# A hybrid decoder layer on one NeuronCore: products with the values in groups of four query blocks

## The chip, the core and the metric

The kernel runs on one core of one Trainium2 chip. The metric is device time in microseconds (us). TensorE multiplies matrices and transposes; the profile shows its matmuls as PE and its weight loads as PEld. VectorE (DVE), ScalarE (ACT) and GpSimd (POOL) work on what it leaves in its banks (PSUM) and on tiles in the core's memory (SBUF). SyncE (SP) and POOL issue DMAs. Each engine works through its own instructions in program order.

## What is computed

One layer on a sequence of 1024 rows of width 1024, all in fp32: a norm, one wide projection, two kinds of attention side by side, an output projection, a norm and the residual. The change touches the first kind, differential attention, with 8 heads:

```python
def diff_attention(q, k, v, lam):
    # q, k: per head two maps of 64 columns; v: per head 128 columns
    ...
        s = jnp.einsum('bqhmd,bkhmd->bhmqk', qb, k).astype(jnp.float32)
        ...
        p = jax.nn.softmax(jnp.where(mask, s, -jnp.inf), axis=-1)
        w = p[:, :, 0] - lam * p[:, :, 1]
        return jnp.einsum('bhqk,bkhv->bqhv', w.astype(v.dtype), v)
...
    oa = rms_norm(oa, subln_g) * (1.0 - lam_init)
    oa = oa.reshape(B, S, DA_WIDTH) * jax.nn.silu(ga)
```

The mask is causal: query row i sees keys 0 to i. So of the 8 x 8 squares of 128 queries by 128 keys that a head has, the 36 on and under the diagonal are computed.

## The kernel before

**Precision.** TensorE is fed with a split of each fp32 factor into a high part (`hi`, rounded to the matmul's type) and the rest (`lo`). A product is three matmuls: hi x hi, lo x hi, hi x lo. ACT makes the high part (a cast), DVE the rest (a subtraction).

**Stages.** Up to about 617 us of the profile the projections run, and the second attention (gated linear attention) beside them. Then comes the stage that the change touches, up to about 933 us, and then the end, which completes the output projection and the last norm.

**The stage.** Three streams share TensorE there, each a Python generator that issues instructions and yields what they cost:

- `all_scores` goes through the heads and, in a head, through the query blocks `qb` from 7 down to 0. `scores(h, qb)` makes the scores of 128 queries against (qb + 1) x 128 keys for both maps (matmuls `sc`), DVE finds each row's extreme while it copies the scores out (a custom instruction, L1167, and a read of its accumulator), ACT takes the exponential with the row sum (L1177), and `scale_scores` joins the maps: DVE a reciprocal (L1202), POOL one product (L1203), DVE the other and the difference (L1207). The result stays in `p0`, one buffer per `qb`; `w[h, qb]` names it.
- `all_values` takes `w` to the products with the values. `values(h, j, ...)` handles the pair of query blocks 2j and 2j + 1. In `turn(g)` TensorE transposes up to four squares of 128 x 128 (two key blocks by two query blocks) into one bank (`wtr`, L114, two banks in rotation, `TR`), ACT casts it to `wt_hi` (L1244) and DVE subtracts to `wt_lo` (L1245). `times(g, ...)` multiplies the two key blocks of v with them: six matmuls into the bank `po`, of 256 columns each, or 128 for the key block that only one of the two query blocks sees. Each turn is issued ahead of the products of the turn before it (`ready`). ACT then copies `po` to half of `o` (L1272). `attn_norm` normalizes `o`, 512 queries at a time: a square and a cast on ACT, a subtraction on DVE (`sq_hl`, L1285), a sum over partitions by two matmuls with ones (`ms`, in the next `TR` bank), a logarithm and an exponential on ACT, products on DVE and POOL, and a store to `mixd`.
- `out_early` multiplies parts of the output projection whose inputs are ready (`ypart`, three matmuls of 512 columns for each step). It waits for nothing of the other two for most of the stage.

**What sets the order.** `merge` holds a clock for each stream and always advances the one that is furthest behind; a stream runs from its begin to its end time (the first two numbers of its list), and each yielded cost moves its clock by that share. A yielded function is a condition that holds a stream back until it is true. So `LAG` sets how far the values follow the scores: 21 of the clock's units, where a head takes 36. `used` tells the scores that a pair's buffers have been read, so that the next head may write them. TensorE's instructions are kept in the order in which they are issued (`mm`, `tr`). The order on ACT, DVE and POOL is settled when the program is built.

Of the kernel before, what the change touches and what calls it, by code (L numbers as in the profile page):

```python
# [14 lines left out]
P = 128  # L15
# [5 lines left out]
DA_HEADS = 8  # L21
# [10 lines left out]
def hymba_kernel(  # L32
# [65 lines left out]
    def bank(i, shape, name):  # L98
        return psum.tile(shape, F32, tag=f"b{i}", name=name)
# [1037 lines left out]
    w, used, scored, opened = {}, set(), [], {}  # L1137

# [73 lines left out]
    def all_scores():  # L1212
        for h in range(DA_HEADS):
            for qb in range(NT - 1, -1, -1):
                if qb % 2 and h:
                    yield lambda h=h, qb=qb: (h - 1, qb // 2) in used
                yield from scores(h, qb)
                if qb == NT - 1 and h + 1 < DA_HEADS:
                    for n, half in (("q", 1), ("k", 0), ("k", 1), ("qs", 1)):
                        load_qk(h + 1, n, half)  # L1220
            if h + 1 < DA_HEADS:
                for n in ("q", "qs"):
                    load_qk(h + 1, n, 0)
        for _ in range(3):
            scale_scores(None)
        scored.append(True)
        opened.update(dict.fromkeys(SC))

    def values(h, j, v, o):

        yield lambda: (h, 2 * j) in w
        po = bank(PO, [P, 256], "po")

        def turn(g):

            n = 512 if g < j else 384
            pt = tr_bank("wtr", [P, 512])
            for c in range(0, n, P):
                t, i = (c // 256, c % 256 // P) if c < 256 or g < j else (1, 1)
                kt = 2 * g + t  # L1240
                tr(pt[:, c : c + P], w[h, 2 * j + i][:, kt * P : (kt + 1) * P])
            hi = smp.tile([P, 512], F32R, tag="wt_hi", name="wt_hi", bufs=3)
            lo = smp.tile([P, 512], F32R, tag="wt_lo", name="wt_lo", bufs=3)
            act.copy(hi[:, :n], pt[:, :n])  # L1244
            dve.tensor_tensor(lo[:, :n], pt[:, :n], fp(hi[:, :n]), ALU.subtract)  # L1245
            return hi, lo

        def times(g, wt):
            hi, lo = wt
            for i, t in ((0, 0), (1, 0), (0, 1), (1, 1), (2, 0), (2, 1)):  # L1250
                a, b = ((v[0], hi), (v[1], hi), (v[0], lo))[i]
                kt = 2 * g + t
                ns = 256 if kt <= 2 * j else P
                mm(
                    po[:, 256 - ns :], a[:, kt, :], b[:, 256 * t : 256 * t + ns],
                    start=(kt == 0 and i == 0), stop=(kt >= 2 * j and i == 2),
                    skip_group_check=True,
                )

        ready = []  # L1260
        for g in range(j + 1):
            ready.append((g, turn(g)))
            if g == j:
                used.add((h, j))
            yield 0.5
            if len(ready) > 1:
                times(*ready.pop(0))
                yield 0.5
        if j == 0:
            yield 0.5  # L1270
        times(*ready.pop(0))
        act.copy(o[:, j % 2 * 256 : j % 2 * 256 + 256], po)  # L1272
        yield 0.5
# [45 lines left out]
    def all_values():  # L1319
        carry = iter(())  # L1320
        nxt = v_first
        for h in range(DA_HEADS):
            v = nxt
            o = [smp.tile([P, 512], F32, tag="o", name="o", bufs=3) for _ in range(2)]
            yield from mingle(values(h, 3, v, o[1]), carry)
            if h + 1 < DA_HEADS:
                nxt = load_v(h + 1)
            yield from values(h, 2, v, o[1])
            yield from mingle(
                chain(values(h, 1, v, o[0]), values(h, 0, v, o[0])), attn_norm(h, 1, o[1])  # L1330
# [170 lines left out]
    def last_times(st, dh, part, e):  # L1501
# [9 lines left out]
    LAG = 21.0  # L1511
# [6 lines left out]
        [LAG, T + LAG, DA_HEADS * 10.5, all_values()],  # L1518
# [128 lines left out]
```

## Time and profile before

| | |
|---|---|
| median of 3 runs | 976.23 us (976.2 to 981.91) |
| the profiled execution's own time | 977.73 us |
| its span, first to last instruction | 976.0 us |
| TensorE clock granted | 0.998 of full speed |
| PE busy | 956.0 us, 98% of the span, 4866 matmuls |
| PEld busy | 806.1 us, 83% |
| DVE busy | 738.7 us, 76% |
| ACT busy | 590.9 us, 61% |
| POOL busy | 211.5 us, 22% |

A matmul's busy time contains its passage through the array, which overlaps with the next one's. What a matmul costs the stream is the time from its start to the start of the next, and that is read from the timeline. A wait of TensorE shows as a wait of PE, or of PEld where the weight load had to wait.

### The profile page before, as it was taken

The numbers are of one execution on the slowest core, as the hardware profiler recorded it, in microseconds if no ns is written. First come the engines' busy times: TensorE is split into PE (matmuls) and PEld (weight loads), VectorE is DVE, ScalarE is ACT, GpSimd is POOL, SyncE is SP. The second block draws the span as 40 slices with busy tenths as digits, with TensorE's granted clock in tenths as the row PEclk, the third lists the DMA queues.
The fourth block names the chain that finished last, engine by engine and source line by source line (L and its number), as shares of the span: only waits on it lengthen the run. The fifth ranks groups of instructions, "written<-read, shape, count | busy, mean of one in ns | idle before, by whom it ended". The sixth has DMA issues, their size and how long they took to land.

```text
span 976.0 us, 14803 instructions
## 1 busy us (share of the span) xinstructions
PE 956.0 (98%) x4866; PEld 806.1 (83%) x4866; DVE 738.7 (76%) x1450; ACT 590.9 (61%) x1152; POOL 211.5 (22%) x289
## 2 busy tenths in 40 slices
PE   6999999999999999999999999999999999999997
PEld 4888888878888888888888888788888888888875
DVE  6996476889889776778787766577787778887655
ACT  8641232347467467766677774357667667787764
POOL 5420100011211221112110000023232233443232
PEclk9999999999999999999999999999999999999999
DMA  8354643768865875899986569997575678995657
GB/s 306 99 152 153 212 134 98 217 174 270 265 240 194 268 250 192 265 280 304 315 278 183 180 204 346 376 337 233 164 252 185 189 267 246 331 262 104 194 157 156
DMA packets 144556, 220.37 MB, mean 226 GB/s; under 512 B 14704, under 2 KB 78704, under 8 KB 144384
## 3 DMA queue, kind: packets, MB, share of 16 engines
q1 hardware_dynamic: 130144, 175.38, 56.6%
q0 software_dynamic: 14336, 44.05, 15.1%
q8 instruction: 38, 0.62, 0.3%
q14 instruction: 38, 0.31, 0.1%
HBM read 133.93 MB, written 88.60 MB: 228 GB/s over the span
## 4 chain that ended last, share of the span: by engine, by line
PE 86%; DMA 6%; DVE 3%; ACT 3%; issue 1%; SPq 1%; DVEq 0%; POOL 0%; ACTq 0%
PE v L111 15%; PE x L111 15%; PE ypart L111 11%; PE y L111 10%; PE z L111 10%; PE sc L111 6%; PE po L111 5%; PE yps L111 4%; PE wtr L114 3%; PE gpo L111 2%; PE kv L111 1%; DMA m_raw<-mixd 1%; DMA m_lo<-mixe 1%; DMA mixd<-o 1%; DMA k_d<-qk_st 1%
## 5 line engine op out<-in xcount | busy, mean ns | idle before, releaser
L1177 ACT ACTIVATE p<-p,stt 128x896 f32<-128x896 f32 (+7 forms) x128 | 99.3, 777 | 46.7 <-DVE stt L1167 43.5
L335 DVE TENSOR_TENSOR w<-w_raw,w 128x512 fp32r<-128x512 f32 x134 | 91.9, 690 | 32.5 <-ACT w L333 32.1
L333 ACT CAST w<-w_raw 128x512 fp32r<-128x512 f32 x134 | 82.5, 620 | 42.9 <-PE y L111 19.9
L1203 POOL TENSOR_SCALAR p<-p,stt,lam 128x1024 f32<-128x1024 f32 (+3 forms) x64 | 55.7, 871 | 209.6 <-DVE stt L1202 203.9
L1167 DVE CUSTOM_DVE_ANT_0 p<-sc,maskt 128x512 f32<-128x512 f32 (+3 forms) x128 | 74.4, 585 | 33.2 <-PE sc L111 32.5
L111 PE MATMUL y<-h_hi,w 128*128 128x512 f32 x320 | 80.6, 394 | 0.0
L111 PE MATMUL x<-s_hi,w 128*128 128x512 f32 x320 | 80.5, 394 | 0.0
L111 PE MATMUL z<-s_hi,w 128*128 128x512 f32 x320 | 80.4, 393 | 0.0
L111 PE MATMUL ypart<-wo_hi,m_hi 128*128 128x512 f32 x192 | 79.5, 414 | 0.6 <-ACT yst L1384 0.5
L111 PE MATMUL v<-w,s_hi 128*128 128x512 f32 x256 | 79.0, 389 | 0.1
L111 PE MATMUL ypart<-wo_hi,m_lo 128*128 128x512 f32 x192 | 75.6, 394 | 0.7 <-DMA m_lo<-mixe 0.7
L111 PE MATMUL ypart<-wo_lo,m_hi 128*128 128x512 f32 x192 | 75.6, 394 | 0.5 <-DMA wo_lo<-wo_d 0.5
L488 ACT COPY s<-x 128x512 f32<-128x512 f32 x60 | 35.0, 584 | 65.2 <-PE x L111 65.0
L111 PE MATMUL sc<-k,q 128*128 128x512 f32 (+1 forms) x192 | 70.9, 372 | 0.4 <-DVE stt L1167 0.4
L111 PEld LDWEIGHTS z<-s_hi,w 128*128 128x128 f32 x320 | 59.1, 188 | 11.6
L111 PEld LDWEIGHTS x<-s_hi,w 128*128 128x128 f32 x320 | 59.1, 188 | 11.7
L111 PEld LDWEIGHTS y<-h_hi,w 128*128 128x128 f32 x320 | 59.0, 188 | 11.6
L111 PE MATMUL sc<-k,qs 128*128 128x512 f32 (+1 forms) x192 | 66.6, 349 | 0.0
L285 ACT CAST w<-w_block 128x1024 fp32r<-128x1024 f32 x24 | 25.0, 1051 | 65.3 <-PE v L111 42.3
L257 DVE TENSOR_TENSOR w_raw<-w_raw 128x512 f32<-128x512 f32 x80 | 55.3, 691 | 9.6 <-DMA w_raw<-in_w_in_dram 8.6
L111 PE MATMUL v<-w,h_hi 128*128 128x512 f32 x192 | 60.0, 400 | 0.4 <-ACT h_hi L582 0.4
L1207 DVE SCALAR_TENSOR_TENSOR p<-p,stt,p 128x1024 f32<-128x1024 f32 (+3 forms) x64 | 52.3, 819 | 6.7 <-POOL p L1203 6.5
(233 smaller groups left out, 2379.8 us busy)
## 6 DMA issues: line engine op xcount, KB each, us to landing
w_raw<-in_w_in_dram SPq DMA_DIRECT2D x40, 512.0 KB, 4.9
w_block<-in_w_in_dram SPq DMA_DIRECT2D x16, 512.0 KB, 4.4
wo_raw<-in_w_out_dram POOLq DMA_DIRECT2D x32, 256.0 KB, 4.2
wo_d<-wo_hi POOLq DMA_DIRECT2D x32, 256.0 KB, 4.5
wo_d<-wo_raw POOLq DMA_DIRECT2D x32, 256.0 KB, 5.0
qs<-q_d SPq DMA_DIRECT2D x32, 256.0 KB, 8.6
k<-k_d SPq DMA_DIRECT2D x16, 512.0 KB, 9.2
q<-q_d SPq DMA_DIRECT2D x16, 512.0 KB, 7.1
```

What stands on the lines that cost most here:

```text
L111: tc.keep_in_program_order(pe.matmul(*a, **k))
L114: tc.keep_in_program_order(pe.transpose(dst, src, ident))
L257: dve.tensor_tensor(dst, a, b, ALU.subtract)
L285: act.copy(w[0], src)
L333: act.copy(w[0], src)
L335: split_last[:] = [dve.tensor_tensor(w[1], src, fp(w[0]), ALU.subtract)]
L488: act.copy(b[k], ps)
L1167: ins = dve.tensor_tensor_reduce(p[:, a:e], sc[:, : e - a], maskt[:, NZ + P - (e - a) :] if last else maskt[:, : e - a], 1.0, 3e38 if i == ...
L1177: act.activation(p[:, :n], p[:, :n], AF.Exp, bias=st[:, m : m + 1], scale=-1.0, accum_out=st[:, 2 + m : 3 + m],)
L1203: pool.tensor_scalar(p1[:, :n], p1[:, :n], st[:, 5:6], lam, ALU.mult, ALU.mult)
L1207: dve.scalar_tensor_tensor(p0[:, :n], p0[:, :n], st[:, 4:5], p1[:, :n], ALU.mult, ALU.subtract)
```

## The change

`values` now takes a half of a head: four query blocks (7 to 4 for `half` 1, 3 to 0 for `half` 0). A turn is one key block `kt`, with up to four transposes, one for each query block that sees it; its products are three matmuls of 512, 384, 256 or 128 columns into a bank of 512. Half 1 has 8 turns (512 columns for key blocks 0 to 4, then 384, 256, 128), half 0 has 4 (512, 384, 256, 128). ACT copies `po` to `o` once for a half, 512 columns.

A half's values may begin when the scores of one more query block have been issued than the half needs (`finished`): half 1 after `qb` 3, half 0 after `qb` 7 of the next head, or when all scores are issued. `used` is set for each half, after its last turn, so the next head's `qb` 7 waits for all of half 1's turns, and its `qb` 3 for all of half 0's. `LAG` becomes 29.5. The costs are now in the clock's own units: half 1 takes `DENSE` = 10 of a head's 36, half 0 the other 26; in the last head each step costs 1.2.

```diff
--- before.py
+++ after.py
@@ -1135,6 +1135,7 @@
 
 
     w, used, scored, opened = {}, set(), [], {}
+    finished = []
 
     def scores(h, qb):
 
@@ -1212,9 +1213,10 @@
     def all_scores():
         for h in range(DA_HEADS):
             for qb in range(NT - 1, -1, -1):
-                if qb % 2 and h:
-                    yield lambda h=h, qb=qb: (h - 1, qb // 2) in used
+                if qb % 4 == 3 and h:
+                    yield lambda h=h, qb=qb: (h - 1, qb // 4) in used
                 yield from scores(h, qb)
+                finished.append(qb)
                 if qb == NT - 1 and h + 1 < DA_HEADS:
                     for n, half in (("q", 1), ("k", 0), ("k", 1), ("qs", 1)):
                         load_qk(h + 1, n, half)
@@ -1226,51 +1228,47 @@
         scored.append(True)
         opened.update(dict.fromkeys(SC))
 
-    def values(h, j, v, o):
-
-        yield lambda: (h, 2 * j) in w
-        po = bank(PO, [P, 256], "po")
-
-        def turn(g):
-
-            n = 512 if g < j else 384
+    def values(h, half, v, o, cost):
+
+        yield lambda: scored or len(finished) > 8 * h + (4 if half else 8)
+        po = bank(PO, [P, 512], "po")
+        last = 4 * half + 3
+
+        def turn(kt):
+
+            first = max(kt - 4 * half, 0)
+            n = 512 - first * P
             pt = tr_bank("wtr", [P, 512])
-            for c in range(0, n, P):
-                t, i = (c // 256, c % 256 // P) if c < 256 or g < j else (1, 1)
-                kt = 2 * g + t
-                tr(pt[:, c : c + P], w[h, 2 * j + i][:, kt * P : (kt + 1) * P])
+            for i in range(first, 4):
+                c = (i - first) * P
+                tr(pt[:, c : c + P], w[h, 4 * half + i][:, kt * P : (kt + 1) * P])
             hi = smp.tile([P, 512], F32R, tag="wt_hi", name="wt_hi", bufs=3)
             lo = smp.tile([P, 512], F32R, tag="wt_lo", name="wt_lo", bufs=3)
             act.copy(hi[:, :n], pt[:, :n])
             dve.tensor_tensor(lo[:, :n], pt[:, :n], fp(hi[:, :n]), ALU.subtract)
-            return hi, lo
-
-        def times(g, wt):
-            hi, lo = wt
-            for i, t in ((0, 0), (1, 0), (0, 1), (1, 1), (2, 0), (2, 1)):
-                a, b = ((v[0], hi), (v[1], hi), (v[0], lo))[i]
-                kt = 2 * g + t
-                ns = 256 if kt <= 2 * j else P
+            return hi, lo, n
+
+        def times(kt, wt):
+            hi, lo, n = wt
+            for i, (a, b) in enumerate(((v[0], hi), (v[1], hi), (v[0], lo))):
                 mm(
-                    po[:, 256 - ns :], a[:, kt, :], b[:, 256 * t : 256 * t + ns],
-                    start=(kt == 0 and i == 0), stop=(kt >= 2 * j and i == 2),
+                    po[:, 512 - n :], a[:, kt, :], b[:, :n],
+                    start=(kt == 0 and i == 0), stop=(kt == last and i == 2),
                     skip_group_check=True,
                 )
 
         ready = []
-        for g in range(j + 1):
-            ready.append((g, turn(g)))
-            if g == j:
-                used.add((h, j))
-            yield 0.5
+        for kt in range(last + 1):
+            ready.append((kt, turn(kt)))
+            if kt == last:
+                used.add((h, half))
+            yield cost
             if len(ready) > 1:
                 times(*ready.pop(0))
-                yield 0.5
-        if j == 0:
-            yield 0.5
+                yield cost
         times(*ready.pop(0))
-        act.copy(o[:, j % 2 * 256 : j % 2 * 256 + 256], po)
-        yield 0.5
+        act.copy(o, po)
+        yield cost
 
     def attn_norm(h, half, o):
         if h < DA_HEADS - 1:
@@ -1322,12 +1320,12 @@
         for h in range(DA_HEADS):
             v = nxt
             o = [smp.tile([P, 512], F32, tag="o", name="o", bufs=3) for _ in range(2)]
-            yield from mingle(values(h, 3, v, o[1]), carry)
+            yield from mingle(values(h, 1, v, o[1], DENSE / 16 if h + 1 < DA_HEADS else 1.2), carry)
             if h + 1 < DA_HEADS:
                 nxt = load_v(h + 1)
-            yield from values(h, 2, v, o[1])
             yield from mingle(
-                chain(values(h, 1, v, o[0]), values(h, 0, v, o[0])), attn_norm(h, 1, o[1])
+                values(h, 0, v, o[0], (36.0 - DENSE) / 8 if h + 1 < DA_HEADS else 1.2),
+                attn_norm(h, 1, o[1]),
             )
             carry = attn_norm(h, 0, o[0])
         last_part(ENDS[0], parts_d[ENDS[0]])
@@ -1508,14 +1506,14 @@
             )
 
     T = 8 * 36.0
-    LAG = 21.0
+    LAG, DENSE = 29.5, 10.0
     s_cost = sum(
         2 * sum(0.08 + (min(b, n) - a) / 512 * 0.56 for a, b in parts_of(n)) + 0.25 + n / 1024 * 1.4
         for n in range(P, S + 1, P)
     )
     merge(
         [0.0, T, DA_HEADS * s_cost, all_scores()],
-        [LAG, T + LAG, DA_HEADS * 10.5, all_values()],
+        [LAG, T + LAG, T, all_values()],
         [-6.0, T + LAG, 11.0 + 14 * 5.52 + 16 * 2.76 + 11.8, out_early()],
     )
 
```

Over 8 heads there are 288 matmuls with values where there were 480, with the same columns in all (110592), the same 288 transposes, 96 turns where there were 80, and 16 copies of `po` where there were 32.

How the order moves is shown at one place, the first turn of the third head (`h` = 2; heads count from 0), on three engines. First TensorE before, from the end of that head's first turn (`wtr_6901`, its third and fourth transpose) to the start of its second (`wtr_6937`). `sc` are scores of the same head's next query block, `ypart` the output projection:

```order
L114 MATMUL wtr_6901<-ident_59,p0_6746 128x128
L114 MATMUL wtr_6901<-ident_59,p0_6658 128x128
L111 MATMUL sc_6910<-k1_6286,q1_6282 128x256
L111 MATMUL sc_6910<-k1_6286,qs1_6288 128x256
L111 MATMUL ypart_6877<-wo_hi_5588,m_hi_6576 128x512
L111 MATMUL ypart_6877<-wo_hi_5588,m_lo_6577 128x512
L111 MATMUL ypart_6877<-wo_lo_5589,m_hi_6576 128x512
L111 MATMUL sc_6918<-k0_6284,q1_6282 128x512
L111 MATMUL sc_6918<-k0_6284,qs1_6288 128x512
L111 MATMUL sc_6922<-k1_6286,q1_6282 128x256
L111 MATMUL sc_6922<-k1_6286,qs1_6288 128x256
L114 MATMUL wtr_6937<-ident_59,p0_6746 128x128
```

And TensorE in the change, from the end of the first turn (`wtr_6918`) over the second turn (`wtr_6942`) to the first product with values (`po_6917`), which reads the first turn:

```order
L114 MATMUL wtr_6918<-ident_59,p0_6706 128x128
L114 MATMUL wtr_6918<-ident_59,p0_6650 128x128
L111 MATMUL sc_6927<-k0_6258,q0_6625 128x384
L111 MATMUL sc_6927<-k0_6258,qs0_6627 128x384
L114 MATMUL wtr_6942<-ident_59,p0_6835 128x128
L114 MATMUL wtr_6942<-ident_59,p0_6790 128x128
L114 MATMUL wtr_6942<-ident_59,p0_6706 128x128
L114 MATMUL wtr_6942<-ident_59,p0_6650 128x128
L111 MATMUL ypart_6848<-wo_hi_5814,m_hi_6552 128x512
L111 MATMUL ypart_6848<-wo_hi_5814,m_lo_6553 128x512
L111 MATMUL ypart_6848<-wo_lo_5815,m_hi_6552 128x512
L111 MATMUL po_6917<-wt_hi_6923,v0_6683 128x512
```

Between the first turn and its products there now stand the scores of one map, a whole turn and one step of the projection. Before, nine matmuls stood between the first two turns alone, and the products with the first came after the second turn and three more. In the change two matmuls of `ms` and then the third turn follow right behind the products.

ACT at the same place before, from the copy of the previous head's last product (`o_6440`) on. `sq_6932` and `sq_hl_6934` belong to that head's norm, `p0_6892` and `p1_6893` to the scores of `qb` 4:

```order
L1272 COPY o_6440<-po_6846 128x256
L1282 ACTIVATE sq_6932<-o_6440 128x512
L1244 CAST wt_hi_6906<-wtr_6901 128x512
L1284 CAST sq_hl_6934<-sq_6932 128x512
L1177 ACTIVATE p0_6892,stt_6891<-p0_6892,stt_6891 128x640
L1244 CAST wt_hi_6942<-wtr_6937 128x512
L1177 ACTIVATE p1_6893,stt_6891<-p1_6893,stt_6891 128x640
```

ACT in the change, from the copy of the previous head's half 0 (`o_6478`) on; `p1_6880` are scores of `qb` 3 and `p0_6908` of `qb` 2:

```order
L1270 COPY o_6478<-po_6712 128x512
L1178 ACTIVATE p1_6880,stt_6878<-p1_6880,stt_6878 128x512
L1280 ACTIVATE sq_6937<-o_6478 128x512
L1282 CAST sq_hl_6939<-sq_6937 128x512
L1247 CAST wt_hi_6923<-wtr_6918 128x512
L1178 ACTIVATE p0_6908,stt_6907<-p0_6908,stt_6907 128x384
L1247 CAST wt_hi_6947<-wtr_6942 128x512
```

The first turn's cast (`wt_hi_6923`) now stands behind an exponential, the square and the norm's cast, and an exponential stands between it and the second turn's.

DVE before: the first turn's subtraction is `wt_lo_6907`, the second's `wt_lo_6943`:

```order
L1167 ISA p0_6892,stt_6891<-sc_6910,maskt_5832,stt_6891 128x128
L1167 ISA stt_6891 128x1
L1207 SCALAR_TENSOR_TENSOR p0_6816<-p0_6816,stt_6815,p1_6817 128x768
L1245 TENSOR_TENSOR wt_lo_6907<-wtr_6901,wt_hi_6906 128x512
L1167 ISA p1_6893,stt_6891<-sc_6918,maskt_5832 128x512
L1167 ISA stt_6891 128x1
L1285 TENSOR_TENSOR sq_hl_6934<-sq_6932,sq_hl_6934 128x512
L1245 TENSOR_TENSOR wt_lo_6943<-wtr_6937,wt_hi_6942 128x512
```

DVE in the change; they are `wt_lo_6924` and `wt_lo_6948`:

```order
L1203 RECIPROCAL stt_6878<-stt_6878 128x2
L1168 ISA p0_6908,stt_6907<-sc_6910,maskt_5832 128x384
L1168 ISA stt_6907 128x1
L1168 ISA p1_6909,stt_6907<-sc_6927,maskt_5832 128x384
L1168 ISA stt_6907 128x1
L1208 SCALAR_TENSOR_TENSOR p0_6879<-p0_6879,stt_6878,p1_6880 128x512
L1283 TENSOR_TENSOR sq_hl_6939<-sq_6937,sq_hl_6939 128x512
L1248 TENSOR_TENSOR wt_lo_6924<-wtr_6918,wt_hi_6923 128x512
L1248 TENSOR_TENSOR wt_lo_6948<-wtr_6942,wt_hi_6947 128x512
```

The first turn's subtraction now stands behind the second map's minimum of `qb` 2 (`p1_6909`), whose scores are issued after the turn's transposes, behind the joining of `qb` 3 (`p0_6879`) and behind the norm's subtraction (`sq_hl_6939`), which before came after it.

## The prediction

> **What bounds the kernel now.** I start with the page's busy times, then look at the stage that the change touches.
>
> ```profile
> PE 956.0 (98%) x4866; PEld 806.1 (83%) x4866; DVE 738.7 (76%) x1450; ACT 590.9 (61%) x1152; POOL 211.5 (22%) x289
> ```
>
> TensorE is the bound, yet 98% says only that matmuls overlap; what is lost shows in its waits. Here are those of the weight loads from the first turn to the last products (637 to 932 us):
>
> ```profile
> PEld po L111 <- DVE wt_lo L1245: 0.9, 4, 0.3
> PEld po L111 <- ACT wt_hi L1244: 0.8, 1, 0.8
> PEld wtr L114 <- ACT r L1295: 0.7, 1, 0.7
> PEld ypart L111 <- ACT yst L1384: 0.7, 1, 0.7
> PEld sc L111 <- DVE stt L1167: 0.6, 1, 0.6
> PEld wtr L114 <- DVE wt_lo L1245: 0.3, 1, 0.3
> ```
>
> They sum to 4.0 us of 295. So the stage is a stream of matmuls that hardly ever waits. Its time changes in two ways: by what the matmuls themselves cost, and by new waits. The first can give little and the second can take much, since nothing is left over.
>
> **Matmuls.** Their cost is the time from start to start in TensorE's timeline; x4 and x2 are merged rows that are labelled by their first shape:
>
> ```profile
> 706.12 0.57 PE L111 MATMUL po<-wt_hi,v 128*128 128x256 f32 x4
> 706.52 0.39 PE L111 MATMUL po<-wt_lo,v 128*128 128x256 f32 x2
> 706.76 0.33 PE L111 MATMUL sc<-k,q 128*128 128x256 f32 x1
> ...
> 712.35 0.60 PE L114 MATMUL wtr<-ident,p 128*128 128x128 f32 x4
> 712.71 0.36 PE L111 MATMUL sc<-k,q 128*128 128x256 f32 x1
> 712.91 0.28 PE L111 MATMUL sc<-k,qs 128*128 128x256 f32 x1
> 713.03 0.40 PE L111 MATMUL ypart<-wo_hi,m_hi 128*128 128x512 f32 x1
> 713.26 0.40 PE L111 MATMUL ypart<-wo_hi,m_lo 128*128 128x512 f32 x1
> ...
> 714.43 0.60 PE L114 MATMUL wtr<-ident,p 128*128 128x128 f32 x4
> ...
> 715.56 0.64 PE L111 MATMUL po<-wt_hi,v 128*128 128x256 f32 x4
> 716.04 0.40 PE L111 MATMUL po<-wt_lo,v 128*128 128x256 f32 x2
> 716.28 0.39 PE L111 MATMUL ypart<-wo_hi,m_hi 128*128 128x512 f32 x1
> ```
>
> Six products of 256 columns take 716.28 - 715.56 = 0.72 us, 0.12 each. One of 512 takes 0.23 (713.03 to 713.26). The group at 706.12 has three of 256 and three of 128 and takes 0.64, so one of 128 takes (0.64 - 0.36) / 3 = 0.09: that is where narrow ones are dear. For 384 I take the middle of 256 and 512, 0.175. Before, a head has six groups of 0.72 and four of 0.64: 6.88 us. In the change it has 18 products of 512, and 6 each of 384, 256 and 128: 4.14 + 1.05 + 0.72 + 0.54 = 6.45. That is 0.43 a head, **3.4 us** over 8 heads; if a 128 that stands alone takes 0.11, as a transpose does, it is 2.5. I take 2.7.
>
> More turns cost TensorE nothing: four transposes take 0.36 and make the next matmul 0.08 longer (0.20 at 712.71 against 0.12), 0.11 a transpose, and their number stays. The 16 additional casts and subtractions lie on ACT and DVE; 16 copies of `po` go. I cost both at nothing by themselves, since ACT is busy 61% and DVE 76%; where they do cost, it is as a wait, next.
>
> On the weight of narrow matmuls the Trainium skill ("TensorE: Matmul & The Clock Gate", Back-to-back issue gap) says more: in streams of weight loads and matmuls it measured some 81 ns for one of 128 columns and 131 ns for one of 512. On a line between these, 256 would take 98 ns, and an estimate from that page would be 12 us less over 8 heads. This trace disagrees: 0.23 us for 512 is twice 0.12 for 256.
>
> **The new waits.** A product waits for its turn's cast (ACT) and subtraction (DVE). These are the rows of ACT, then DVE, at the third head's first turn before, whose transposes are those at 712.35 above:
>
> ```profile
> 712.22 0.35 ACT L1272 COPY o<-po 128x256 f32<-128x256 f32 x1
> 712.67 0.64 ACT L1282 ACTIVATE sq<-o 128x512 f32<-128x512 f32 x1
> 713.21 0.56 ACT L1244 CAST wt_hi<-wtr 128x512 fp32r<-128x512 f32 x1
> 713.67 0.62 ACT L1284 CAST sq_hl<-sq 128x512 fp32r<-128x512 f32 x1
> 714.19 0.83 ACT L1177 ACTIVATE p<-p,stt 128x640 f32<-128x640 f32 x1
> ```
>
> ```profile
> 713.67 1.02 DVE L1207 SCALAR_TENSOR_TENSOR p<-p,stt,p 128x768 f32<-128x768 f32 x1
> 714.61 0.68 DVE L1245 TENSOR_TENSOR wt_lo<-wtr,wt_hi 128x512 fp32r<-128x512 f32 x1
> ...
> 715.81 0.69 DVE L1285 TENSOR_TENSOR sq_hl<-sq,sq_hl 128x512 fp32r<-128x512 f32 x1
> 716.42 0.68 DVE L1245 TENSOR_TENSOR wt_lo<-wtr,wt_hi 128x512 fp32r<-128x512 f32 x1
> ```
>
> The transposes end at 712.35 + 0.44 = 712.79, the subtraction at 715.29: 2.5 us later, and the products that need it start at 716.04. So before it is 0.75 us early. In the change's order less stands between. With zero at the start of the first turn: transposes to 0.44, two scores of 384 to 0.79, the second turn to 1.23, three steps of `ypart` to 1.92, two products with `wt_hi` to 2.38. There the third product needs `wt_lo`, **1.94 us** behind the transposes. With the old delay of 2.5 it would wait 0.56.
>
> The delay grows too, since more stands in front on both engines. For that I need four more durations, each the mean of a group in the stage:
>
> ```profile
> L1177 ACT ACTIVATE p<-p,stt 128x512 f32<-128x512 f32 x16 | 11.5, 720 | 2.7 <-DVE stt L1202 1.3 <-DVE stt L1167 1.2
> L1384 ACT COPY yst<-ypart 128x512 f32<-128x512 f32 x30 | 17.4, 583 | 6.0 <-PE ypart L111 5.2 <-ACT p L1177 0.4
> L1167 DVE CUSTOM_DVE_ANT_0 p<-sc,maskt 128x384 f32<-128x384 f32 x16 | 8.7, 548 | 1.0 <-PE sc L111 1.0
> L1207 DVE SCALAR_TENSOR_TENSOR p<-p,stt,p 128x512 f32<-128x512 f32 x8 | 6.4, 794 | 0.1
> ```
>
> Instructions that follow each other start about 0.08 us before the one ahead ends (713.67 + 1.02 against 714.61), so I take 0.08 off each. On ACT: the last product of the head before ends 1.74 us ahead of zero, for by the program's order six matmuls of 512 and two of 384 stand between. The copy of 512 columns then runs to -1.24, the exponential to -0.48 (with its accumulator's read about its full 0.72 and a little), the square to 0.06, the norm's cast to 0.58, the turn's cast to 1.04. On DVE: the second map's scores end at 0.79, so their minimum ends at 1.34 (its read of the accumulator fills the overlap), the joining of `qb` 3 at 2.05, the norm's subtraction at 2.66, the turn's at 3.34. That is **0.96 us** past 2.38, hand-offs between engines left out. The second turn's subtraction ends at about 3.94, and the third turn, which needs its bank, stands at 3.34 + 0.23 + 0.46 = 4.03 behind the product and `ms`: no second wait here. DVE, not ACT, comes last; while it does, `ms`, the third turn, and all scores and steps of `ypart` behind it wait on TensorE.
>
> The same place comes in each head. The first has no norm in front, the last has more distance; in the fourth and fifth the engines hold still more ahead. I take 1.0 us a head, **8.0** in all. The ends: nothing, as a bare cast and subtraction (0.56 + 0.68) fit into 1.94; and 2.0 a head if hand-offs and the orders of the fourth and fifth head count everywhere, 16.
>
> Of the old waits, 4.0 us, those for late products and for the end should partly go; I take 2.0 (ends 0 and 4.0).
>
> **What moves without a price.** A half's result is stored to `mixd` later, as the values lag more. Its readers stand on the chain that ended last, at
>
> ```profile
> 786.67 5.46 DMA mixd<-o
> 792.19 3.60 DMA m_raw<-mixd
> ```
>
> By the program's order the first matmul on that load stands about 6 us of matmuls further behind the store's `ms` than before, so these 9 us stay covered; uncovered, they would cost at most 9. SP issues the same loads and stores, and the values' next load lies a head ahead of its use. The next head's first scores now wait for all turns of half 1; these stand ahead of them on TensorE anyway.
>
> **Sum.** 977.73 (the profiled execution's own time; its span is 976.0) - 2.7 - 2.0 + 8.0 = 981.0. The median of the runs, 976.23, is 1.5 below that execution, which makes **979.5 us**. A measurement of this kernel tells about 1%, 9.8 us, from no change; I forecast no change, on the slow side.
>
> **Rivals.**
>
> *The delay is absorbed.* If the engines reach the first turn with nothing queued, waits sum to 0 to 2.5 us: 977.73 - 1.5 - 2.7 - 2 to 4 + 0 to 2.5, **969.5 to 974**. For it: a quarter of DVE's time is idle, and the old waits are few. Against it: the old delay of 2.5 us already exceeds 1.94.
>
> *Slower: half 1 as a whole runs at DVE's pace.* In the five turns after the first the program's order leaves 2.0 to 2.8 us between transposes and third product. Before, the second turn's subtraction ended at 717.10, 2.23 us behind its transposes (714.43 + 0.44). One more instruction of 0.6 in front would put it past most of these. At 0.35 us for each of five turns in 8 heads that is 14 us on top of my sum: **993.5**. It decides from a delay of about 2.6 us. Against it: the first wait gives both engines time to catch up.
>
> *Wide matmuls are cheaper by the column.* If each of the 192 matmuls that go gave back at least what one of 128 columns takes, 0.09 us, that is 17 us: 977.73 - 1.5 - 17 = **959**. The rows above speak against it: two of 256 cost what one of 512 does. The rule of the Trainium skill ("TensorE: Matmul & The Clock Gate", Back-to-back issue gap) points this way.
>
> **Chances.** Forecast (976 to 984) 0.56, absorbed 0.28, DVE's pace 0.13, wide matmuls 0.02, other 0.01. Faster by over 1% is under 966.5: 0.02 for the wide matmuls. Slower by over 1% is over 986: 0.13. The rest, 0.85, is the same. The range runs from 970, which takes in most of the absorbed case, to 988, which takes in the forecast with half as much wait again and leaves most of DVE's pace out.
>
> **What would show it.** Right: `po` with 288 matmuls; the weight loads' wait of `po` for `wt_lo` at some 8 us, about one wait of 1 us in each head, at its first turn; `wt_lo`'s end over 2.4 us behind those transposes. Absorbed: that wait stays at 1 to 2 us in all. DVE's pace: 16 us or more, several a head. Wrong altogether: if a wait on `mixd` or on `w` (transposes held by the joining of `qb` 4) led the list, or if a product of 512 took other than 0.23.

## The result, and the profile after

The changed kernel takes 992.34 us (median, 990.1 to 992.95), the kernel before 977.85 on the same chip: a ratio of 1.0135, 95% interval 1.0113 to 1.0157. That is 13 us slower by the ratio (14.5 by the two medians), where no change was forecast (979.5). The profiled execution took 990.1 us with a span of 988.4, 12.4 longer than before.

The page's busy times of the changed kernel:

```profile
PE 956.0 (97%) x4674; PEld 792.8 (80%) x4674; DVE 748.0 (76%) x1466; ACT 587.3 (59%) x1152; POOL 211.1 (21%) x289
```

There are 192 matmuls fewer, as planned, and PE's busy time is the same to the tenth. So the 12.4 us are not work but idle time. The view by windows shows where it lies; the columns are the window's length, the busy times of PE, PEld, DVE, ACT and POOL, and the clock granted. First before, one window and the sum of four from 616 to 970 us, then the changed kernel, from 616 to 982:

```profile
700.00:800.00 100.00, 99.89 (x585) 87.03 (x584) 74.95 (x203) 67.82 (x149) 30.04 (x33) 1.00 0.61 202
...
sum 354.00, PE 349.85 PEld 299.85 DVE 256.36 ACT 240.33 POOL 117.39; mean PE 87.46 PEld 74.96 DVE 64.09 ACT 60.08 POOL 29.35
```

```profile
700.00:800.00 100.00, 95.24 (x495) 78.64 (x493) 78.12 (x210) 65.93 (x148) 30.21 (x34) 1.00 0.59 188
...
sum 366.00, PE 349.62 PEld 285.77 DVE 265.30 ACT 236.65 POOL 117.68; mean PE 87.40 PEld 71.44 DVE 66.32 ACT 59.16 POOL 29.42
```

PE idled 354.00 - 349.85 = 4.2 us of the stage before and 366.00 - 349.62 = 16.4 now, at the full clock in both. The difference, 12.2, is the loss of the profiled execution. The view of waits says on what; this is the weight loads' list for 637 to 950 us (before, in the prediction, for 637 to 932):

```profile
PEld po L111 <- DVE wt_lo L1248: 15.3, 15, 1.9
PEld wtr L114 <- DVE p L1208: 5.1, 6, 2.1
PEld sc L111 <- DVE stt L1168: 3.1, 4, 1.3
PEld po L111 <- ACT wt_hi L1247: 2.1, 4, 0.8
PEld wtr L114 <- DVE wt_lo L1248: 1.9, 2, 1.1
PEld ypart L111 <- ACT yst L1382: 0.5, 1, 0.5
```

28.0 us where it was 4.0 (a weight load waits earlier than its matmul, so not all of it is lost). Products wait for `wt_lo`, as forecast, but for twice as long. To place them I summed TensorE's stretches from start to start beyond a matmul's usual pitch, by turn: half 1's first turn 6.3 us (10 places), the third turn behind it 1.3, **half 0's first turn 5.1** (4 places), **the first transposes of a head, waiting for a joining, 3.9** (6), scores 2.5, the rest 2.0: 21.2 in all, against 3.9 before.

The timeline of TensorE and DVE at the fifth head's half 1 shows the forecast place:

```profile
796.88 0.66 PE L114 MATMUL wtr<-ident,p 128*128 128x128 f32 x4 [0.57 <-DVE p L1208]
...
797.66 1.13 DVE L1283 TENSOR_TENSOR sq_hl<-sq,sq_hl 128x512 fp32r<-128x512 f32 x1 [0.28 <-ACT sq_hl L1282]
...
798.71 0.74 DVE L1208 SCALAR_TENSOR_TENSOR p<-p,stt,p 128x512 f32<-128x512 f32 x1
798.78 0.72 PE L111 MATMUL po<-wt_hi,v 128*128 128x512 f32 x2
...
799.85 1.28 DVE L1248 TENSOR_TENSOR wt_lo<-wtr,wt_hi 128x512 fp32r<-128x512 f32 x2
...
800.58 0.50 PE L111 MATMUL po<-wt_lo,v 128*128 128x512 f32 x1 [1.08 <-DVE wt_lo L1248]
```

The transposes end at 796.88 + 0.44 = 797.32. TensorE is ready for the product with `wt_lo` at 798.78 + 0.32 + 0.23 = 799.33 (a product of 512 takes 0.23, and some 0.08 more right behind transposes), so it **has** 2.0 us; DVE, with the norm's subtraction, a joining and a minimum (799.37, not shown) ahead, **needs** until 799.85 + 0.68 = 800.53, 3.2 us. The subtraction itself takes 1.13 us here where the median of the 16 is 0.69; it ends 0.54 behind a product `p` of POOL (797.48, 0.77 us). The last section comes back to that. Now the second head's half 0, which I had not priced:

```profile
699.79 0.92 PE L114 MATMUL wtr<-ident,p 128*128 128x128 f32 x7
...
701.65 1.28 DVE L1208 SCALAR_TENSOR_TENSOR p<-p,stt,p 128x1024 f32<-128x1024 f32 x1
702.06 0.62 PE L111 MATMUL po<-wt_hi,v 128*128 128x512 f32 x2
702.85 0.68 DVE L1283 TENSOR_TENSOR sq_hl<-sq,sq_hl 128x512 fp32r<-128x512 f32 x1
703.45 1.14 DVE L1248 TENSOR_TENSOR wt_lo<-wtr,wt_hi 128x512 fp32r<-128x512 f32 x2
704.19 0.50 PE L111 MATMUL po<-wt_lo,v 128*128 128x512 f32 x1 [1.50 <-DVE wt_lo L1248]
```

The same queue, with a joining of 1024 columns (1.28 us) in it, since half 0 begins behind the next head's `qb` 7. It has 702.52 - 700.23 = 2.3 us and needs 3.9.

### The profile page after: what moved, and what is told of

Its sections match the earlier page's. It is cut to its first block, busy times and chain, and to the rows that moved or that the text cites. A ratio compares the mean times of both kernels' runs of the same rounds, so it can differ in the third digit from the quotient of the medians.

```text
span 988.4 us, 14441 instructions
## 1 busy us (share of the span) xinstructions
PE 956.0 (97%) x4674; PEld 792.8 (80%) x4674; DVE 748.0 (76%) x1466; ACT 587.3 (59%) x1152; POOL 211.1 (21%) x289
## 4 chain that ended last, share of the span: by engine, by line
PE 85%; DVE 5%; issue 3%; DMA 3%; ACT 2%; POOL 1%; DVEq 0%; SPq 0%; POOLq 0%; ACTq 0%
PE x L111 17%; PE v L111 15%; PE y L111 11%; PE z L111 11%; PE ypart L111 8%; PE sc L111 5%; PE yps L111 4%; PE po L111 4%; PE gpo L111 3%; PE wtr L114 2%; DVE p L1208 1%; PE kv L111 1%; DVE p L1168 1%; DMA qs<-q_d 1%; POOL p L1204 1%
## 5 line engine op out<-in xcount | busy, mean ns | idle before, releaser
L1248 DVE TENSOR_TENSOR wt_lo<-wtr,wt_hi 128x512 fp32r<-128x512 f32 (+1 forms) x96 | 52.3, 552 | 20.2 <-ACT wt_hi L1247 19.4
L1208 DVE SCALAR_TENSOR_TENSOR p<-p,stt,p 128x1024 f32<-128x1024 f32 (+3 forms) x64 | 55.9, 874 | 14.3 <-POOL p L1204 14.2
L257 DVE TENSOR_TENSOR w_raw<-w_raw 128x512 f32<-128x512 f32 x80 | 55.2, 690 | 10.6 <-DMA w_raw<-in_w_in_dram 9.6
```

Source lines behind the costliest of these rows:

```text
L257: dve.tensor_tensor(dst, a, b, ALU.subtract)
L1208: dve.scalar_tensor_tensor(p0[:, :n], p0[:, :n], st[:, 4:5], p1[:, :n], ALU.mult, ALU.subtract)
```

## The experiments

Three theories are tried. **Queue:** the loss is DVE's queue ahead of the first turns, and goes when `wt_lo` gets more time. **Shape:** matmuls of 512 columns are themselves the loss. **Lag:** the later begin is. Ratios are to the kernel before on the same chip; the change itself stands at 1.0135. All edits are to the changed kernel where nothing else is said.

**e1: the products cut into pieces of at most 256 columns.** It leaves one product out, that of the lower columns of key block 0 with the first part.

```diff
-                mm(
-                    po[:, 512 - n :], a[:, kt, :], b[:, :n],
+                for c in range(0, n, 256):
+                    e = min(c + 256, n)
+                    mm(
+                        po[:, 512 - n + c : 512 - n + e], a[:, kt, :], b[:, c:e],
...
```

> The change with each product with values cut into pieces of at most 256 columns, all else as it is. Queue theory (the 14 us come from products and transposes that are issued too close behind what ACT and DVE must finish, at the first turn of half 1, at the first turn of half 0 and at the transposes that need the last block's w; the wide form itself is harmless): 992.3 plus the 2 to 3 us that the narrow pieces cost, less what the waits swallow, so 992 to 995. Shape theory (wide products, or turns over four blocks, are slow by themselves): the time falls towards the kernel before, 985 or less.

Measured: 1002.61 us, ratio 1.024 (1.0191 to 1.0289), above the 992 to 995 of Queue too. Shape fell: narrow pieces are some 10 us slower still. b6 below puts about half of that on the pieces themselves, with a wide interval. The weight loads' waits sum to little more than in the change, 29 us against 28 (less for `wt_lo`, 11.5, and more for joinings, 6.5, and for `wt_hi`, 4.6). But two waits of TensorE, 1.99 and 2.93 us, came with 3.4 and 6.8 us at half the clock (0.50 in the windows 849.70:853.10 and 935.00:941.80), which cost the profiled execution, the slowest of the four, some 5 us.

**e2: the norm's subtraction (`sq_hl`) behind the last turn's `wt_lo`.**

```diff
-            dve.tensor_tensor(lo[:, :n], pt[:, :n], fp(hi[:, :n]), ALU.subtract)
+            turned[:] = [dve.tensor_tensor(lo[:, :n], pt[:, :n], fp(hi[:, :n]), ALU.subtract)]
...
-        dve.tensor_tensor(hl[:, 1], sq, fp(hl[:, 0]), ALU.subtract)
+        with tc.issue_after(turned[0].ins):
+            dve.tensor_tensor(hl[:, 1], sq, fp(hl[:, 0]), ALU.subtract)
```

> The change with the norm's subtraction on DVE (sq_hl) held behind the subtraction of the turn that is issued last before it; TensorE's order stays. Queue theory: the first turns wait some 0.6 us less each where that subtraction stood in front, about ten places, so 986 to 988, with the wait of po for wt_lo at 9 to 11 us instead of 15.3; the sum of squares (ms) may take part of it back. Shape theory: 992.

Measured: 992.48 us, ratio 1.0134 (1.0106 to 1.0163): nothing gained, where Queue had said 986 to 988. Its waits:

```profile
PEld po L111 <- DVE wt_lo L1248: 11.3, 15, 1.5
PEld wtr L114 <- DVE p L1208: 9.2, 6, 3.4
PEld ms L111 <- DVE sq_hl L1284: 2.2, 5, 0.9
```

The queue is there: `wt_lo` waits less by 4.0 us. But the 0.68 us now stand ahead of a joining and of `ms`, which wait 4.1 and 2.2 longer. Another order of DVE's queue moves the wait; it does not remove it.

**e3: more distance.** 1.5 clock units more behind the first turn of each half and a pause of 6 ahead of half 0, taken from half 0's steps, so that a head keeps its length.

```diff
+        if not half and h + 1 < DA_HEADS:
+            yield 6.0
...
-            yield cost
+            yield cost if kt else cost + 1.5
...
-                values(h, 0, v, o[0], (36.0 - DENSE) / 8 if h + 1 < DA_HEADS else 1.2),
+                values(h, 0, v, o[0], (36.0 - DENSE - 9.0) / 8 if h + 1 < DA_HEADS else 1.2),
```

> The change with 1.5 units of the clock more behind the first turn of each half, and a pause of 6 units ahead of half 0 (taken from its later steps), so that other matmuls stand between the first turn and its products: 2.9 us instead of 2.0 to the third product in half 1, 5.2 instead of 2.3 to 3.0 in half 0. Queue theory: the first turn of half 1 loses about 5 of its 7.6 us and that of half 0 its 5 us; the transposes' wait for w stays: 982 to 984. Shape theory: 991 to 993.

Measured: 979.97 us, ratio 1.0006 (0.9984 to 1.0029). The whole loss is gone, with products of the same width and the same `LAG`. So neither the width nor the later begin by itself is the loss in this form, and Queue gives back more than expected.

**e6 and e7: which half?** e6 gives half 1's first turn alone 1.5 units more (half 0's steps shortened by as much), e7 half 0 alone its pause and its 1.5.

```diff
-            yield cost
+            yield cost if kt or not half else cost + 1.5
```

> The changed kernel, with 1.5 clock units more behind the first turn of half 1 alone, and half 0's eight steps shorter by as much in sum, so that the heads keep their length. Theory (the loss is a sum of queues at single places, and each place can be mended by itself): the first product of half 1's first turn, which waited 6.3 us in all, and the third turn's bank behind it (1.3 us) come free; half 0's first turn (5.1 us) and the transposes that wait for the joining (3.9 us) stay: 984 to 987. Rival (the loss moves to the next place when one is mended, as with the norm's subtraction moved behind): 990 to 993.

Measured: 981.45 us, ratio 1.0038 (1.0018 to 1.0057), better than the theory's 984 to 987.

```diff
+        if not half and h + 1 < DA_HEADS:
+            yield 6.0
...
-            yield cost
+            yield cost if kt or half else cost + 1.5
```

> The changed kernel, with a pause of 6 clock units ahead of half 0 and 1.5 more behind its first turn, and its eight steps shorter by 7.5 in sum; half 1 as in the changed kernel. Theory (a sum of places): half 0's first turn gives back 4 to 5 us, half 1's first turn keeps its 6.3: 986 to 988.5; with the run of half 1 alone the two gains add up to that of both together, 12.4 us. Rival (moved on): 990 to 993. A second rival (half 0's pause is what matters, since it lets VectorE empty its queue once a head): 980 to 983.

Measured: 985.22 us, ratio 1.0077 (1.0053 to 1.01): a gain of some 6 us, and half 1's first turn keeps 6.6 us of stretches. e6 gained some 9.5, more than the 7.6 that half 1's first turn and the third behind it had cost. The two gains sum to 15, that of e3 is 12.6: they do not simply add up. The timeline of e6 at the two places shown above:

```profile
791.15 0.60 PE L114 MATMUL wtr<-ident,p 128*128 128x128 f32 x4
...
793.32 0.69 DVE L1248 TENSOR_TENSOR wt_lo<-wtr,wt_hi 128x512 fp32r<-128x512 f32 x1
...
793.92 0.74 DVE L1208 SCALAR_TENSOR_TENSOR p<-p,stt,p 128x512 f32<-128x512 f32 x1
794.01 0.62 PE L111 MATMUL po<-wt_hi,v 128*128 128x512 f32 x2
794.47 0.39 PE L111 MATMUL po<-wt_lo,v 128*128 128x512 f32 x1
794.58 0.68 DVE L1283 TENSOR_TENSOR sq_hl<-sq,sq_hl 128x512 fp32r<-128x512 f32 x1
```

```profile
699.11 0.93 PE L114 MATMUL wtr<-ident,p 128*128 128x128 f32 x7
...
700.97 1.28 DVE L1208 SCALAR_TENSOR_TENSOR p<-p,stt,p 128x1024 f32<-128x1024 f32 x1
702.17 0.69 DVE L1248 TENSOR_TENSOR wt_lo<-wtr,wt_hi 128x512 fp32r<-128x512 f32 x1
702.40 0.62 PE L111 MATMUL po<-wt_hi,v 128*128 128x512 f32 x2
702.77 0.68 DVE L1283 TENSOR_TENSOR sq_hl<-sq,sq_hl 128x512 fp32r<-128x512 f32 x1
702.91 0.50 PE L111 MATMUL po<-wt_lo,v 128*128 128x512 f32 x1
```

Two things changed at once. TensorE comes later: it has 2.9 and 3.3 us instead of 2.0 and 2.3. And in the order that was built DVE does `wt_lo` ahead of the norm's subtraction, at the first place ahead of the joining too: it needs 2.4 and 3.3. The second gain came in half 0 as well, whose steps e6 only shortened; TensorE's order is made of slots, and a product there landed one slot later. Not all is gained: in e6 transposes wait 4.2 us for `ms`, in six places, where the change has no such wait.

**e9: 0.5 units instead of e6's 1.5.** The edit is e6's.

> The changed kernel, with 0.5 clock units more behind half 1's first turn (1.5 in the run that took 981.5 us). Theory (the waits fall with the distance between a first turn's transposes and its product with wt_lo): 0.5 units is less than one slot of TensorE's order, so the product goes one slot later in only some of the heads; a third to a half of the gain, 986 to 989. Rival (the heads' steps against the joinings decide, a matter of phase and not of distance): either no gain, 991 to 993, or the whole of it, 981 to 983.

Measured: 990.85 us, ratio 1.0145 (1.0126 to 1.0165): no gain, the first rival's side. Its waits:

```profile
PEld po L111 <- DVE wt_lo L1248: 13.7, 14, 1.7
PEld wtr L114 <- DVE p L1208: 7.1, 5, 2.9
```

Here are the means of the first seven heads, worked out from the timelines as at the two places above (us: from the transposes' end to the end of `wt_lo`; to the time when TensorE is ready for it; the product's delay):

| | half 1: needs | has | waits | half 0: needs | has | waits |
|---|---|---|---|---|---|---|
| the change | 2.80 | 2.05 | 0.80 | 3.18 | 2.70 | 0.73 |
| e9 (0.5 units) | 2.82 | 2.18 | 0.70 | 3.06 | 2.90 | 0.54 |
| e6 (1.5 units) | 2.43 | 2.96 | 0.07 | 2.55 | 3.55 | 0.01 |
| e7 (half 0) | 2.84 | 2.28 | 0.63 | 2.94 | 5.09 | 0.00 |
| e3 (both) | 2.69 | 2.89 | 0.20 | 2.43 | 4.99 | 0.00 |

e9's 0.5 units bought 0.13 and 0.20 us of distance on average, since in each half the product moved by a slot in two heads of seven, and hardly in the others. The small gain in `wt_lo`'s wait went to the joinings. Through all five rows the wait follows needs against has; e9 alone does not tell whether distance or DVE's order does more.

**e4: the change with `LAG` 32.0 instead of 29.5.**

> The change with the values 2.5 units later (LAG 32.0). By the order the transposes stand 6.4 us behind the last block's scores instead of 4.7, and half 0's first products 4.0 to 4.7 us behind their turn instead of 2.3 to 3.0; half 1's stay at 2.1. Queue theory: the wait for w (5.1) and that at half 0's first turn (about 5) go, that at half 1's first turn (about 7.6) stays: 982 to 984. Shape theory: 992. Third possibility (the next head's scores, which wait for half 1's turns, are what costs): 994 or more.

Measured: 985.9 us, ratio 1.0067 (1.0046 to 1.0087), above the 982 to 984 of Queue. Half 0's waits went, and a new kind came. ACT, then TensorE, in its timeline:

```profile
796.96 0.62 ACT L1358 CAST m_hi<-m_raw 128x512 fp32r<-128x512 f32 x1 [2.21 <-DMA m_raw<-mixd]
```

```profile
800.01 0.63 PE L114 MATMUL wtr<-ident,p 128*128 128x128 f32 x4 [3.06 <-DVE wt_lo L1248]
```

With the stores 2.5 units later, ACT's queue stands still for a load of `mixd`, turn casts included, and TensorE with it. That is the cover that the prediction left without a price; at 29.5 it still holds.

**e5: the kernel before with only `LAG` 29.5.** Does the lag alone cost anything?

> The kernel before (pairs of query blocks) with LAG 29.5 instead of 21.0, nothing else. If a later start by itself costs nothing: 976 to 980, as before. If lag itself is what costs (later stores, held scores): 983 or more.

Measured: 992.59 us, ratio 1.0137 (1.0107 to 1.0168), as slow as the change; 976 to 980 was to show a harmless lag. Its timeline at the longest wait (DVE, POOL, PE):

```profile
829.15 3.50 DVE L1361 TENSOR_TENSOR m_lo<-m_raw,m_hi 128x512 fp32r<-128x512 f32 x1
...
829.61 1.64 POOL L1299 TENSOR_TENSOR o<-r,gate 128x512 f32<-128x512 f32 x1
...
830.88 1.21 POOL L1203 TENSOR_SCALAR p<-p,stt,lam 128x640 f32<-128x640 f32 x1
...
833.77 0.69 PE L111 MATMUL po<-wt_lo,v 128*128 128x256 f32 x2 [3.12 <-DVE wt_lo L1245]
```

A subtraction that takes 0.69 us elsewhere takes 3.50 and ends (832.65) 0.56 us behind POOL's second product (832.09). A second one, at 874.02, takes 2.12 and ends 0.56 behind POOL as well. Both stand ahead of a `wt_lo` (the first with a minimum between). So I tried:

**e8: e5 with the product `o<-r,gate` on DVE instead of POOL.**

```diff
-        pool.tensor_tensor(dst, r, gate, ALU.mult)
+        dve.tensor_tensor(dst, r, gate, ALU.mult)
```

> The kernel before with its values begun 8.5 units later (LAG 29.5), as in the run that took 992.6 us, and the product with the gate (o<-r,gate, 14 of them) on VectorE instead of GpSimd. Theory (the later start cost its 14 us because two subtractions m_lo on VectorE started beside that product on GpSimd and ended 0.56 us after GpSimd's last one, 3.5 and 2.1 us instead of 0.69, so that two products waited 3.3 us each and the matmuls behind each wait ran 0.2 us longer for some 6 us): 978 to 982, and no m_lo above 1 us. Rival (the later start itself, by held scores and later stores, costs it): 988 to 993.

Measured: 998.31 us, ratio 1.0213 (1.0188 to 1.0238). No `m_lo` exceeds 0.91 us, but the time rose. TensorE's longest wait now is

```profile
820.74 0.79 PE L111 MATMUL ypart<-wo_hi,m_hi 128*128 128x512 f32 x1 [6.80 <-ACT m_hi L1360]
```

for a cast whose load of `m_raw` took 11.5 us from issue to landing (before, the first such load took 6.5). The stretched subtraction was the wait of e5, not the reason that a later begin is dear in the old form: there, something else is late next. Why that form bears no later begin stays open.

**Is there a version that beats both?** The edits of e3 with `LAG` 32.0:

> The spread first turns (980.0 alone) and the later start (LAG 32.0, 985.9 alone) together. Queue theory: the transposes' wait for w, 3 to 4 us of the spread kernel's remaining 10, goes, and its first turns' rest shrinks: 975 to 978. Rival (the later start holds up the next head's scores, which wait until half 1's turns are issued): 981 or more.

980.94 us, ratio 1.0029 (1.0012 to 1.0046). With the norm begun two steps later besides (two `yield 0.0` ahead of `sq`):

> As the one with both, and the norm of the half before starts two steps of the values later (in all heads but the last), so that its square, cast and subtraction are not issued between the first turn and its products. Queue theory: 974 to 977, at or a little below the one with both; the sum of squares now stands nearer to the fourth turn's bank, which may take 1 to 2 us back. Rival: no gain over the one with both.

979.13 us, 1.0011 (0.9995 to 1.0028). With e8's edit on top:

> The spread values with LAG 32 and the norm two steps later (979.1 us), and the product with the gate on VectorE. Theory: that run's two waits of over 1 us on wt_lo (1.6 us at 832.5 and 1.05 us at 800.1) each stood behind a VectorE operation that was stretched beside GpSimd's product with the gate (m_lo 2.15 instead of 0.69 us, p 1.95 instead of 1.10); they go, and VectorE's 0.69 us more per half stands two steps behind a turn: 975.5 to 977.5, which would beat both kernels. Rival (0.69 us more in VectorE's queue holds up joinings and turns at 14 places): 979 to 983.

978.87 us, 0.9995 (0.9973 to 1.0016). The same as c1 with `LAG` 30.5, and c1 with e6's edit in place of e3's and `LAG` 31.0:

> Values spread in both halves, the norm two steps later, the product with the gate on VectorE, LAG 30.5 instead of 32.0 (978.9 us). Theory (what is left is TensorE's wait on y's bank and on ms, 1.7 and 1.2 us, which a head that begins 1.5 units earlier need not have): 975.5 to 978. Rival (the joining of the fourth query block is then late for the transposes again): 979 to 982.

> 1.5 units more behind half 1's first turn alone, the norm two steps later, the product with the gate on VectorE, LAG 31.0. Theory: against the run with 1.5 units in half 1 alone (981.5 us) the transposes' waits on the joining (4.2 us, two places) and on ms (4.2 us, six places) mostly go: 975.5 to 978.5. Rival (half 0's eight steps, 3.1 units each, leave VectorE's first turn there no room): 980 to 983.

984.96 us, 1.008 (1.0064 to 1.0097), and 985.75 us, 1.0087 (1.0069 to 1.0104). None of the five reached its forecast, and none beats the kernel before; the best equals it. c1's list shows what is left:

```profile
PEld po L111 <- DVE wt_lo L1250: 4.1, 9, 0.8
PEld wtr L114 <- DVE wt_lo L1250: 2.5, 4, 1.4
PEld sc L111 <- DVE stt L1168: 2.3, 7, 0.3
PEld ypart L111 <- ACT yst L1387: 2.2, 2, 1.7
```

Many small waits at different places: the stretches from start to start sum to 7.7 us against 3.9 before, in an execution that took 982.7, some 4 us over the median. The difference is about as large as what the products save.

**How much do wide products save by themselves?** b6 is b1 with pieces of at most 256 columns (all of them multiplied in):

> The one with both, its products cut into pieces of at most 256 columns. This is the worth of wide products where few waits are left. By the start-to-start times 2 to 3 us more than the one with both. If the 10 us that narrow pieces cost in the change itself are their own: 10 more.

985.4 us, 1.0079 (1.0053 to 1.0105), against b1's 1.0029: 0.0050 of 978, about 5 us (the intervals leave 1 to 9). In the two traces the products with values, from each one's start to the start of the next matmul, sum to 58.3 and 55.2 us, 3.1 apart; in the kernel before it is 57.2.

## Why the prediction was wrong, point by point

- **Matmuls, -2.7:** the direction was right, and `po` has 288 matmuls. The size stays open between 1 and 9: b6 against b1 gives 5 by time and 3.1 by the rows, and before against b1 2.0 by the rows (57.2 and 55.2). By places the stretches grew by 17.3 us and the span by 12.4; how much of the 4.9 between them is this term is not shown.
- **The wait at half 1's first turn, +8.0: right in place and size**, 6.3 and 1.3 behind it, 7.6 us. At the place that was walked, the third head, DVE needs 2.99 us and TensorE has 1.95, where the prediction had 2.90 and 1.94. That the sum fits so well is luck in part. The first head, which was to wait little for want of a norm in front, waited 1.18, the seventh 0.16; and the third turn, which was not to wait, did so in two heads (the 1.3).
- **Half 0's first turn, no price: the step that failed first**, +5.1. I walked one place in DVE's order and took half 0, which runs at 3.25 units a step, for slack. But a step's width does not move the first product out of the way: it stood 2.3 to 3.0 us behind its transposes, and the joining of 1024 columns came just there. By the sum the span was to grow by 3.3 us; it grew by 12.4. This place (5.1) and the next bullet's transposes (3.9), neither with a price, make 9.0 of the 9.1 that were missing; what else was off about cancels.
- **The transposes' wait for `w`, no price: the second step that failed.** The prediction named it only as a sign of being wrong. A head's first transposes now stand close behind the scores of `qb` 4, which pass DVE, ACT and POOL before DVE joins them: they waited 5.1 us for `p` (PEld; 3.9 by the stretches), where the list of before had none. A full queue on DVE is not all of it: at the longest, 2.15 us, DVE had stood idle for 0.81 shortly before the joining, until an exponential of ACT ended (837.68).
- **"These stand ahead of them on TensorE anyway": held.** No wait of DVE for half 1's transposes shows. The scores that do wait are those of later blocks of a head (`qb` 5 and 4), and they wait for DVE: for `stt` 3.1 us where it was 0.6, in four places, each shortly behind a joining of 896 columns that took 1.79 to 2.17 us where 1.15 is usual. The last section shows one.
- **Old waits, -2.0:** they did not go; that of the scores for `stt` is one of them.
- **`mixd` without a price:** right at `LAG` 29.5; e4 and e8 show the price when it is not covered.
- **The profiled execution against the median, -1.5:** I carried the offset over. After, the median lies 2.2 above its own profiled execution. This makes 3.7 of the 12.8 us by which I was off. The offset came from three runs; with a fourth the median of before is 977.85, and it is gone.
- **The rivals:** "DVE's pace" gave 993.5 but for a reason that did not occur: the middle turns of half 1 hardly waited (1.0 us of TensorE's idle time in two places, the third turn's), and the delay past which I had let it decide, 2.6, was passed (2.80). The time came out near by another way. "Absorbed" fell, and "cheaper by the column" too: 0.23 us for 512 columns stands.

## What to carry to other kernels

When a change makes work start together that was spread before, walk the queue of the engine that hands over at **every** place where it starts, not at the one that looks tightest, and write down what it needs against what it has; here two more places cost as much as the one I had walked. Price a removed instruction only after that: 192 matmuls were worth some 2 to 5 us, and three queues at the heads' turns cost more. In e2 a wait cured by another order on a busy engine came back at its next customer. In e3 and e6 distance, once it was a whole slot, took away more than came back. Whether the distance or DVE's order that came with it did more is not shown.

## What the hardware showed besides

**The clock can drop behind a wait.** These are windows of e5 ahead of, behind and further behind its wait of 3.12 us (the clock granted stands third from the right), then of e8 right behind its 6.80, and of e1 shortly behind a wait of 1.99:

```profile
824.00:830.00 6.00, 6.00 (x33) 5.09 (x32) 4.46 (x12) 5.29 (x12) 4.08 (x6) 1.00 0.79 192
833.70:840.10 6.40, 6.33 (x22) 5.53 (x23) 2.78 (x8) 3.83 (x9) 1.68 (x2) 0.52 1.03 401
840.10:846.00 5.90, 5.90 (x39) 5.21 (x38) 4.86 (x17) 4.85 (x14) 1.57 (x2) 1.00 0.46 101
```

```profile
820.70:824.40 3.70, 3.66 (x9) 2.64 (x10) 1.76 (x3) 0.99 (x2) 0.00 (x0) 0.50 0.31 96
```

```profile
849.70:853.10 3.40, 3.40 (x14) 2.93 (x12) 2.60 (x8) 1.52 (x4) 1.20 (x2) 0.50 1.05 337
```

In these 3 to 6 us a matmul takes about twice its time, so e5's wait of 3.12 us costs about 6. The wait need not be that long: 1.99 us were enough in e1, and in e4 the clock stood at 0.50 from 879.60 to 883.00 around a wait of 1.43. In the changed kernel the longest wait of TensorE in the stage is 1.72 us (838.68), and its clock stays at 1.00; this is no part of its loss. What decides is not shown by these runs. The Trainium skill ("TensorE: Matmul & The Clock Gate", What's actually happening) says that the clock goes to half after an idle window of some 3.4 us and comes back after a busy one of the same length. Half the clock agrees with 0.50 and 0.52; the length does not: 3.12 us and less were enough here, and the return took up to 6.4.

**DVE waits for POOL.** The 3.50 us of `m_lo` above fit a rule of the Trainium skill ("SBUF — State Buffer", Who interferes with whom): a DVE instruction with two inputs in SBUF contends with a POOL instruction that reads SBUF. This trace agrees for that form: it ends 0.56 us behind POOL's two products, and e8, which took one of them off POOL, has none over 0.91.

The changed kernel has it too. This is the joining of the fifth head's `qb` 6 (896 columns), POOL's product with the gate, and the scores of `qb` 5 that wait until DVE is through with its next minimum:

```profile
787.38 1.80 DVE L1208 SCALAR_TENSOR_TENSOR p<-p,stt,p 128x896 f32<-128x896 f32 x1
786.92 1.30 POOL L1297 TENSOR_TENSOR o<-r,gate 128x512 f32<-128x512 f32 x1 [0.62 <-DVE r L1295]
789.63 0.50 PE L111 MATMUL sc<-k,q 128*128 128x512 f32 x1 [0.38 <-DVE stt L1168]
```

The joining ends at 789.18, 0.96 behind POOL's 788.22. Four of the eight joinings of 896 columns started behind that product like this, and took 1.79 to 2.17 us; one that started 0.17 ahead of it (749.10 against 749.27) took its 1.15. In c1, where that product is on DVE, all eight take 1.15. Which of the two must be first is not settled: in e5 the 3.50 us start ahead of POOL's product by the rows (829.15 against 829.61).
